# RG-LRU gates on 64 rows and two heads at a time, and weight sums of the LRU groups split during the second MLP product

## The chip, the cores and the metric

The kernel runs on one core of one Trainium2 chip. The metric is the device time of one execution in microseconds (us). The engines are TensorE (PE in the profile; PEld is its loading of weights), VectorE (DVE), ScalarE (ACT), GpSimd (POOL) and SyncE (SP, which here only issues transfers). Each engine works through its own instructions in order.

## The reference

One decoder block over 2048 tokens of width 1024, all in float32. Two mixers work side by side on one projection of the normed input, a gated short convolution (512 channels) and the Griffin block (1024 channels); after them come an output projection and an MLP of width 4096.

```python
h = rmsnorm(x, norm_mix_g)
gate_b, gate_c, v, x_r, g = split(h @ w_in)         # 512, 512, 512, 1024, 1024
y_conv = gate_b * causal_dwconv(gate_c * v, conv_w)           # 3 taps
xr = causal_dwconv(x_r, rnn_conv_w) + rnn_conv_b              # 4 taps
r = sigmoid(block_diag_linear(xr, w_a, b_a))        # 16 heads of 64 x 64
i = sigmoid(block_diag_linear(xr, w_x, b_x))
log_a = -8 * r * softplus(-lam)
a = exp(log_a)
bx = sqrt(-expm1(2 * log_a)) * (i * xr)
y_rnn = scan(h[t] = a[t] * h[t-1] + bx[t]) * gelu(g)
x = x + concat(rmsnorm(y_conv), rmsnorm(y_rnn)) @ w_out
x = x + relu(rmsnorm(x) @ w_mlp_in)^2 @ w_mlp_out
out = rmsnorm(x)
```

## The kernel before

**Products.** Each float32 operand is split into a rounded part `hi` (a cast on ACT, L166) and the remainder `lo` (a subtraction on DVE, L167), and each product is three passes over the array: hi by hi, hi by lo and lo by hi (`passes`). In the names of the profile, `w_hi` and `w_lo` are such parts of a weight, `xr_hi` and `xr_lo` those of the convolved x_r, `z_hi` those of the MLP's hidden values. One matmul multiplies 128 rows by 128 columns of weights and moves 512 tokens.

**Stages.** The tokens are worked in two halves of 1024. The first half runs `mixers_plain` (to about 420 us), the output projection, the first MLP product (`Up`), and the second one (`Down`, 822 to 1127 us, 56 steps of 24 matmuls, or 5.45 us). `Up`, `Down` and the second half's projection use a scheme of seven products in place of eight, whose order is `ORDER = (1, 2, 6, 5, 7, 3, 4)`. The second half runs `mixers_blocks` (1127 to about 1440 us), then the same stages.

**Weights of the second half.** The seven-product scheme needs four blocks of W_in in each of seven groups (groups 0 to 3 are the Griffin block's, each with x_r and g of two channel units; 4 and 5 belong to the convolution; 6 is its gate) and four sums of them. The first half leaves them in DRAM: products 1, 2 and 4 of a group as split pairs (`d_ws`), the sums of products 7, 5, 6 and 3 unsplit (`d_wk`). `mixers_blocks` fetches a split pair on POOL's queue (`wr`, three products ahead) and an unsplit sum on SP's (`wk`, four ahead), which it then splits two products ahead on ACT and DVE.

**The gates.** One unit is 128 channels, two heads. `Lru.conv` makes xr of four taps, the first on ACT (L492) and three on DVE (L500), and splits it. `Lru.gate` holds the gate matrices of the unit as 128 x 128 blocks with zeros off the diagonal: for w_a and w_x, for two blocks of 512 tokens, three passes, so 12 matmuls into two PSUM tiles `psri` (L513); then a sigmoid for each (L522, L523). `Lru.scan` follows: tanh, exp, square root on ACT, several products on DVE, one addition of 1 on ACT (L533), the scan on DVE (L537), and a copy of its state on POOL (L538). There are eight units in each half, 16 gates in all.

**Order.** PE's order is the order of the code. The other engines' orders and the transfers' are set by a scheduler at build time; tiles come from pools of fixed size, and a load or a result waits until the tile it takes over is free. In the second half the table `STEPS` puts a group's gates between the products of the next group: the first gate after product 1, its scan after 2, the second gate after 6, so two products (10.9 us) lie between them. For the first group another table applies: first gate after product 6, second after 5, one product (5.45 us) between. In the text, "group 1" means the products of group 1, with group 0's gates among them, and so on to group 4.

Of the kernel before, what the change touches and what calls it, by code (L numbers as in the profile page):

```python
# [8 lines left out]
F32 = mybir.dt.float32  # L9
F32R = mybir.dt.float32r  # L10
# [49 lines left out]
def block_kernel(  # L60
# [154 lines left out]
    def passes(s, m):  # L215
        return [(s[0], m[0]), (s[0], m[1]), (s[1], m[0])]
# [81 lines left out]
    def par(nm, i):  # L298
        return prm[:, off[nm] + i : off[nm] + i + 1]
# [182 lines left out]
    class Lru:  # L482
# [6 lines left out]
        def conv(self, xin):  # L489
            c, j = self.c, self.j  # L490
            xr = self.new("xr", (P, 2 * TB))
            nc.scalar.activation(  # L492
                xr,
                xin[:, j, 0 : 2 * TB],
                AF.Identity,
                bias=par("rnn_conv_b", c),
                scale=par("rnn_conv_w", c),
            )
            for k in range(1, 4):
                V.scalar_tensor_tensor(  # L500
                    xr, xin[:, j, k : k + 2 * TB], par("rnn_conv_w", 8 * k + c), xr, MUL, ADD
                )
            self.xr = xr
            self.split = split_new(xr, self.new, "xr")

        def gate(self, gw):
            c, j = self.c, self.j
            ps = [psum("psri") for _ in range(2)]
            for g in range(2):
                for blk in range(2):  # L510
                    pl = passes(gw, self.split)
                    for i, (ws, xs) in enumerate(pl):
                        nc.tensor.matmul(  # L513
                            ps[g][:, blk, :],
                            ws[:, j, g, :],
                            xs[:, blk * TB : blk * TB + TB],
                            start=i == 0,
                            stop=i == len(pl) - 1,
                        )
            self.r = temp("r")  # L520
            self.gi = self.new("gi")
            nc.scalar.activation(self.r, ps[0], AF.Sigmoid, bias=par("b_a", c))  # L522
            nc.scalar.activation(self.gi, ps[1], AF.Sigmoid, bias=par("b_x", c))  # L523

        def scan(self):
            c = self.c
            r, gi = (t.rearrange("p b s -> p (b s)") for t in (self.r, self.gi))
            V.tensor_mul(gi, gi, self.xr)
            v = self.xr
            nc.scalar.activation(v, r, AF.Tanh, scale=sp4[:, c : c + 1])  # L530
            nc.scalar.activation(r, r, AF.Exp, scale=sp8[:, c : c + 1])
            V.scalar_tensor_tensor(v, r, 1.0, v, ADD, MUL)
            nc.scalar.activation(r, v, AF.Identity, bias=ones[:, 0:1])  # L533
            V.scalar_tensor_tensor(v, v, 2.0, v, ADD, MUL)
            nc.scalar.activation(v, v, AF.Sqrt, scale=-1.0)
            V.tensor_mul(gi, gi, v)
            V.tensor_tensor_scan(v, r, gi, state[:, c, :], MUL, ADD)  # L537
            nc.gpsimd.tensor_copy(state[:, c, :], v[:, 2 * TB - 1 : 2 * TB])  # L538
            self.v, self.y = v, gi
# [11 lines left out]
        return acc  # L551

    def load_gate(pr):
        raw = gp.tile([P, 2, 2, P], F32, name="gate_raw")
        nc.gpsimd.dma_start(raw, gate_w[:, 2 * pr : 2 * pr + 2])
        t = temp("gate", (P, 2, 2, 2, P), F32R)
        s = (t[:, 0], t[:, 1])
        round_off(s[0], raw, s[1])
        return s
# [81 lines left out]
    def keep_sums(n):  # L641
        for i, t in weight_sums(*rawkept.pop(n)).items():
            kept[n, i] = spill("wk", t)

    def mixers_plain(h):
        acc = None
# [83 lines left out]
    class In:  # L730
# [5 lines left out]

        def fetch(self, i):
            ds = kept.pop((self.n, i))
            if i in (1, 2, 4):
                self.ready[i] = [wtile("wr", WSHAPE, F32R) for _ in range(2)]  # L740
                for t, d in zip(self.ready[i], ds):
                    nc.gpsimd.dma_start(t, d)
            else:
                self.raw[i] = refill("wk", ds, wtile)
# [113 lines left out]
    def mixers_blocks(H, more):  # L858
# [6 lines left out]
        ysB = []  # L865
        for n in range(-FETCHW, len(seq)):
            for m, sums in ((n + FETCHW, True), (n + FETCHW - 1, False)):
                if 0 <= m < len(seq) and (seq[m][1] not in (1, 2, 4)) == sums:
                    G[seq[m][0]].fetch(seq[m][1])
            m = n + LEADW  # L870
            if 0 <= m < len(seq):
                G[seq[m][0]].prepare(seq[m][1])
            if n < 0:
                continue
            s, i = seq[n]
            if s == 6 and i == 1:
                G[6].us = [G[4].u, G[5].u]
            G[s].multiply(i, H)
            G[s].drain(i)
            more(n)  # L880
            if 1 <= s <= 4:
                p = G[s - 1]
                for step in ({6: (0,), 5: (1, 2), 7: (3, 4)} if s == 1 else STEPS).get(i, ()):
                    if step == 0:
                        p.units[0].gate(p.gw)
                        p.units[1].conv(p.xin)
                    elif step == 1:
                        p.units[0].scan()
                    elif step == 2:
                        p.units[1].gate(p.gw)  # L890
                        y, acc = p.units[0].out(p.g, acc)
                        ysB.append(y)
                    elif step == 3:
                        p.units[1].scan()
                    else:
                        y, acc = p.units[1].out(p.g, acc)
                        ysB.append(y)
            if s == 6 and i == 6:
                rB = stats(acc, D, "B")
                fetched = [fetch_y(ysB, pr, 0) for pr in range(2)]  # L900
            if s == 6 and i == 7:
                early = split_y(fetched[0], "g_norm_rnn", 0)
            if s == 6 and i == 3:
                accA = conv_out(G[4].u, accA)
# [309 lines left out]
    for b in range(0, NB, 2):  # L1214
# [45 lines left out]
        with tc.manual_schedule(engines={nc.tensor.engine}):  # L1260
# [52 lines left out]
            for n in range(len(dseq) - (0 if more else 2)):  # L1313
# [14 lines left out]
                if (i, a) == (4, 0):  # L1328
                    finish(b)
                if more:  # L1330
                    if (i, a) == (5, 0):
                        load_xt(2)
                        ops2 = Operands()
# [60 lines left out]
def _lay_out(inputs):  # L1394
    import numpy as _np

    a = {n: _np.asarray(inputs[n]) for n in _INS}
    a["x_t"] = a["x"][0].T
    a["params"] = _np.concatenate([a[n].reshape(-1, P) for n, _ in ROWS]).T
    g = _np.zeros((P, NLRU, 2, P), _np.float32)  # L1400
    for n, nm in enumerate(("w_a", "w_x")):
        w = a[nm][0].reshape(NLRU, 2, 64, 64)
        for e in range(2):
            s = slice(64 * e, 64 * e + 64)
            g[s, :, n, s] = w[:, e].transpose(1, 0, 2)
    a["gate_w"] = g
    return a

# [22 lines left out]
```

## Time and profile before

| what | value |
|---|---|
| runs | 2208.73, 2209.22, 2214.24 us; median 2209.22 |
| profiled execution | 2209.43 us, of which the span of the profile is 2207.7 |
| granted clock of PE | 0.994 |
| busy: PE, weight loads, DVE, ACT, POOL | 97%, 80%, 66%, 45%, 6% of the span |
| matmuls | 9514, of them 192 at the gates |
| moved between DRAM and the core | 432 MB, 196 GB/s on average |

Busy time of PE counts a matmul from its start to its modelled end, and matmuls overlap, so the time of a row of them is read from their starts. An idle time in brackets behind a row of the timeline is that of its engine just before, with what ended it. "ACT xr_hi L166" as a releaser means that the engine waited for the cast of xr.

### The profile page before, as it was taken

The numbers are of one execution on the slowest core, as the hardware profiler recorded it, in microseconds if no ns is written. First come the engines' busy times: TensorE is split into PE (matmuls) and PEld (weight loads), VectorE is DVE, ScalarE is ACT, GpSimd is POOL, SyncE is SP. The second block draws the span as 40 slices with busy tenths as digits, with TensorE's granted clock in tenths as the row PEclk, the third lists the DMA queues.
The fourth block names the chain that finished last, engine by engine and source line by source line (L and its number), as shares of the span: only waits on it lengthen the run. The fifth ranks groups of instructions, "written<-read, shape, count | busy, mean of one in ns | idle before, by whom it ended". The sixth has DMA issues, their size and how long they took to land. (4 is left out here: it accounts for less than half of the span.)

```text
span 2207.7 us, 24962 instructions
## 1 busy us (share of the span) xinstructions
PE 2148.5 (97%) x9514; PEld 1773.1 (80%) x9514; DVE 1461.3 (66%) x1707; ACT 996.3 (45%) x1239; POOL 129.0 (6%) x224
## 2 busy tenths in 40 slices
PE   6999999999999999999999999999999999999998
PEld 5788787888887888888887778878878888888886
DVE  6577764669877785467675878456887575654446
ACT  5687813345323334343446876244543323433333
POOL 0021110000111110000010111000000000000000
PEclk9999999999999999999999999999999999999999
DMA  9654655431786788386462334655135344876431
GB/s 338 215 178 142 238 209 178 167 134 59 276 304 253 287 310 344 140 319 224 157 220 91 137 125 145 219 189 181 43 120 191 137 173 150 321 288 234 165 143 77
DMA packets 170632, 431.62 MB, mean 196 GB/s; under 512 B 14352, under 2 KB 63504, under 8 KB 170512
## 3 DMA queue, kind: packets, MB, share of 16 engines
q1 hardware_dynamic: 146416, 346.12, 43.8%
q0 software_dynamic: 21216, 74.46, 9.2%
q10 hardware_dynamic: 2880, 9.44, 1.1%
q8 instruction: 75, 1.23, 0.2%
q14 instruction: 45, 0.37, 0.0%
HBM read 292.60 MB, written 137.36 MB: 195 GB/s over the span
## 5 line engine op out<-in xcount | busy, mean ns | idle before, releaser
L770 PE MATMUL up<-H,w_hi 128*128 128x512 f32 x1792 | 554.2, 391 | 3.6 <-DVE snap L962 3.4
L167 DVE TENSOR_TENSOR w_lo<-w,w_hi 128x1024 fp32r<-128x1024 f32 x208 | 253.7, 1223 | 222.2 <-issue 120.7
L770 PEld LDWEIGHTS up<-H,w_hi 128*128 128x128 f32 x1792 | 336.8, 188 | 74.2 <-ACT H L166 4.2
L770 PE MATMUL up<-H,w_lo 128*128 128x512 f32 x896 | 350.0, 391 | 3.9 <-DVE w_lo L167 3.9
L1056 PE MATMUL dn<-w_hi,z_hi 128*128 128x512 f32 x896 | 349.7, 390 | 1.6 <-DVE x L1371 1.6
L1056 PE MATMUL dn<-w_lo,z_hi 128*128 128x512 f32 x896 | 349.3, 390 | 0.4 <-DVE w_lo L167 0.4
L1056 PE MATMUL dn<-w_hi,z_lo 128*128 128x512 f32 x896 | 349.1, 390 | 0.0
L166 ACT CAST w_hi<-w 128x1024 fp32r<-128x1024 f32 x208 | 216.5, 1050 | 195.1 <-PE dn L1056 143.3
L167 DVE TENSOR_TENSOR z_lo<-z,z_hi 128x1024 fp32r<-128x1024 f32 x112 | 136.9, 1222 | 112.1 <-issue 88.9
L770 PEld LDWEIGHTS up<-H,w_lo 128*128 128x128 f32 x896 | 168.7, 188 | 39.0 <-DVE w_lo L167 4.3
L1056 PEld LDWEIGHTS dn<-w_hi,z_hi 128*128 128x128 f32 x896 | 168.3, 188 | 37.1 <-DVE x L1371 2.4
L1056 PEld LDWEIGHTS dn<-w_lo,z_hi 128*128 128x128 f32 x896 | 168.3, 188 | 36.3 <-DVE w_lo L167 1.2
L1056 PEld LDWEIGHTS dn<-w_hi,z_lo 128*128 128x128 f32 x896 | 168.3, 188 | 35.1
L166 ACT CAST z_hi<-z 128x1024 fp32r<-128x1024 f32 x112 | 117.7, 1051 | 167.7 <-PE dn L1056 157.1
L167 DVE TENSOR_TENSOR w_lo<-raw,w_hi 128x1024 fp32r<-128x1024 f32 x76 | 92.8, 1223 | 95.3 <-ACT w_hi L166 59.5
L166 ACT CAST w_hi<-raw 128x1024 fp32r<-128x1024 f32 x76 | 79.7, 1053 | 168.7 <-PE po L241 86.7
L770 PE MATMUL in<-H,w_hi 128*128 128x512 f32 x448 | 138.7, 391 | 0.0
L949 ACT COPY snap<-up 128x1024 f32<-128x1024 f32 x48 | 48.7, 1014 | 181.1 <-PE up L770 171.1
L241 PE MATMUL po<-w_hi,y_hi 128*128 128x512 f32 x384 | 120.2, 395 | 3.5 <-ACT y_hi L621 3.5
L241 PE MATMUL po<-w_hi,y_lo 128*128 128x512 f32 x384 | 119.1, 391 | 0.2
L241 PE MATMUL po<-w_lo,y_hi 128*128 128x512 f32 x384 | 119.1, 392 | 0.0
L770 PE MATMUL in<-H,wr 128*128 128x512 f32 x504 | 116.0, 390 | 0.0
(247 smaller groups left out, 3260.0 us busy)
## 6 DMA issues: line engine op xcount, KB each, us to landing
z<-d_z SPq DMA_DIRECT2D x112, 512.0 KB, 6.7
w<-in_w_mlp_out_dram SPq DMA_DIRECT2D x80, 512.0 KB, 5.9
w<-in_w_mlp_in_dram SPq DMA_DIRECT2D x64, 512.0 KB, 4.7
d_z<-snap SPq DMA_DIRECT2D x64, 512.0 KB, 2.9
w<-d_w SPq DMA_DIRECT2D x64, 512.0 KB, 4.4
raw<-in_w_out_dram SPq DMA_DIRECT2D x48, 512.0 KB, 3.8
d_z<-z SPq DMA_DIRECT2D x48, 512.0 KB, 2.8
wr<-d_ws POOLq DMA_DIRECT2D x42, 512.0 KB, 5.3
```

What stands on the lines that cost most here:

```text
L166: nc.scalar.copy(hi, src)
L167: latest[0] = V.tensor_tensor(lo, src, hi.bitcast(F32), SUB).ins
L241: nc.tensor.matmul(ps[:, half, :], ys[:, j, t * P : (t + 1) * P], ws[j][:, 0, half * 512 : (half + 1) * 512], start=first and i == 0, stop ...
L770: nc.tensor.matmul(ps[:, j, :], ws[:, k, j * P : (j + 1) * P], hs(k), start=i in (1, 2, 5) and k == 0 and n == 0, stop=k == 3 and n == len ...
L949: nc.scalar.copy(t, ps)
L1056: nc.tensor.matmul(ps[t // 2][:, t % 2, :], zs[:, p, t * P : (t + 1) * P], ws[:, p, :], start=i in (1, 2, 5) and a == 0 and p == 0 and n == 0,
```

## The change

1. `conv`: the first tap goes from ACT to DVE, as one instruction that multiplies and adds.
2. `gate`: the matrices of one head become a 64 x 128 block, 64 columns of w_a and 64 of w_x. The two heads lie in rows 0 to 63 and 64 to 127 of the array, and each has a PSUM tile of its own. Still 12 matmuls of 512 tokens for a unit, each on 64 rows, those of the two heads next to each other.
3. Since head 0's tile has w_a's outputs in its first 64 partitions and w_x's in the others, and head 1's the other way round, there are four sigmoids on 64 partitions each, in place of two on 128. The biases of w_x are stored turned by 64.
4. The gate weights take half the memory: 128 KB a load in place of 256, and casts and remainders of 256 columns in place of 512.
5. `scan`: the addition of 1 goes from ACT to DVE.
6. `split_sums`: in the first half's second MLP product, after every third step from step 2 to step 47, one of the 16 sums of groups 0 to 3 is loaded back (SP, 512 KB), split (ACT cast, DVE subtraction) and stored as a pair (two stores of 512 KB on POOL's queue). In `mixers_blocks` these 16 then come as split pairs on POOL's queue, 32 loads in place of 16 on SP's, three products ahead, with no split there.

```diff
--- before.py
+++ after.py
@@ -489,12 +489,8 @@
         def conv(self, xin):
             c, j = self.c, self.j
             xr = self.new("xr", (P, 2 * TB))
-            nc.scalar.activation(
-                xr,
-                xin[:, j, 0 : 2 * TB],
-                AF.Identity,
-                bias=par("rnn_conv_b", c),
-                scale=par("rnn_conv_w", c),
+            V.tensor_scalar(
+                xr, xin[:, j, 0 : 2 * TB], par("rnn_conv_w", c), par("rnn_conv_b", c), MUL, ADD
             )
             for k in range(1, 4):
                 V.scalar_tensor_tensor(
@@ -506,21 +502,28 @@
         def gate(self, gw):
             c, j = self.c, self.j
             ps = [psum("psri") for _ in range(2)]
-            for g in range(2):
-                for blk in range(2):
-                    pl = passes(gw, self.split)
-                    for i, (ws, xs) in enumerate(pl):
+            head = [slice(0, 64), slice(64, P)]
+            pl = passes(gw, self.split)
+            for blk in range(2):
+                for i, (ws, xs) in enumerate(pl):
+                    for e in range(2):
                         nc.tensor.matmul(
-                            ps[g][:, blk, :],
-                            ws[:, j, g, :],
-                            xs[:, blk * TB : blk * TB + TB],
+                            ps[e][:, blk, :],
+                            ws[head[e], j, :],
+                            xs[head[e], blk * TB : blk * TB + TB],
                             start=i == 0,
                             stop=i == len(pl) - 1,
                         )
             self.r = temp("r")
             self.gi = self.new("gi")
-            nc.scalar.activation(self.r, ps[0], AF.Sigmoid, bias=par("b_a", c))
-            nc.scalar.activation(self.gi, ps[1], AF.Sigmoid, bias=par("b_x", c))
+            for e in range(2):
+                own, other = head[e], head[1 - e]
+                nc.scalar.activation(
+                    self.r[own], ps[e][own], AF.Sigmoid, bias=par("b_a", c)[own]
+                )
+                nc.scalar.activation(
+                    self.gi[own], ps[e][other], AF.Sigmoid, bias=par("b_x", c)[other]
+                )
 
         def scan(self):
             c = self.c
@@ -530,7 +533,7 @@
             nc.scalar.activation(v, r, AF.Tanh, scale=sp4[:, c : c + 1])
             nc.scalar.activation(r, r, AF.Exp, scale=sp8[:, c : c + 1])
             V.scalar_tensor_tensor(v, r, 1.0, v, ADD, MUL)
-            nc.scalar.activation(r, v, AF.Identity, bias=ones[:, 0:1])
+            V.tensor_scalar(r, v, 1.0, None, ADD)
             V.scalar_tensor_tensor(v, v, 2.0, v, ADD, MUL)
             nc.scalar.activation(v, v, AF.Sqrt, scale=-1.0)
             V.tensor_mul(gi, gi, v)
@@ -551,9 +554,9 @@
         return acc
 
     def load_gate(pr):
-        raw = gp.tile([P, 2, 2, P], F32, name="gate_raw")
+        raw = gp.tile([P, 2, P], F32, name="gate_raw")
         nc.gpsimd.dma_start(raw, gate_w[:, 2 * pr : 2 * pr + 2])
-        t = temp("gate", (P, 2, 2, 2, P), F32R)
+        t = temp("gate", (P, 2, 2, P), F32R)
         s = (t[:, 0], t[:, 1])
         round_off(s[0], raw, s[1])
         return s
@@ -641,6 +644,11 @@
     def keep_sums(n):
         for i, t in weight_sums(*rawkept.pop(n)).items():
             kept[n, i] = spill("wk", t)
+
+    def split_sums(k):
+        key = (k // 4, (7, 5, 6, 3)[k % 4])
+        t = refill("wk", kept[key])
+        kept[key] = [spill_r("ws", r, nc.gpsimd) for r in split_new(t, temp, "w")]
 
     def mixers_plain(h):
         acc = None
@@ -736,7 +744,7 @@
 
         def fetch(self, i):
             ds = kept.pop((self.n, i))
-            if i in (1, 2, 4):
+            if isinstance(ds, list):
                 self.ready[i] = [wtile("wr", WSHAPE, F32R) for _ in range(2)]
                 for t, d in zip(self.ready[i], ds):
                     nc.gpsimd.dma_start(t, d)
@@ -865,7 +873,7 @@
         ysB = []
         for n in range(-FETCHW, len(seq)):
             for m, sums in ((n + FETCHW, True), (n + FETCHW - 1, False)):
-                if 0 <= m < len(seq) and (seq[m][1] not in (1, 2, 4)) == sums:
+                if 0 <= m < len(seq) and (seq[m][0] > 3 and seq[m][1] not in (1, 2, 4)) == sums:
                     G[seq[m][0]].fetch(seq[m][1])
             m = n + LEADW
             if 0 <= m < len(seq):
@@ -1328,6 +1336,8 @@
                 if (i, a) == (4, 0):
                     finish(b)
                 if more:
+                    if n % 3 == 2 and n < 48:
+                        split_sums(n // 3)
                     if (i, a) == (5, 0):
                         load_xt(2)
                         ops2 = Operands()
@@ -1396,13 +1406,15 @@
 
     a = {n: _np.asarray(inputs[n]) for n in _INS}
     a["x_t"] = a["x"][0].T
-    a["params"] = _np.concatenate([a[n].reshape(-1, P) for n, _ in ROWS]).T
-    g = _np.zeros((P, NLRU, 2, P), _np.float32)
+    rows = {n: a[n].reshape(-1, P) for n, _ in ROWS}
+    rows["b_x"] = _np.roll(rows["b_x"], 64, axis=1)
+    a["params"] = _np.concatenate([rows[n] for n, _ in ROWS]).T
+    g = _np.zeros((P, NLRU, P), _np.float32)
     for n, nm in enumerate(("w_a", "w_x")):
         w = a[nm][0].reshape(NLRU, 2, 64, 64)
         for e in range(2):
-            s = slice(64 * e, 64 * e + 64)
-            g[s, :, n, s] = w[:, e].transpose(1, 0, 2)
+            f = e ^ n
+            g[64 * e : 64 * e + 64, :, 64 * f : 64 * f + 64] = w[:, e].transpose(1, 0, 2)
     a["gate_w"] = g
     return a
 
```

How it moves instructions, at three places. First PE at the second gate of the first half, between products of x_r (`ps_x`; `h_hi`, `h_lo` are the normed input's parts). Before:

```order
L222 MATMUL ps_x<-h_lo,w_hi 128x512
L222 MATMUL ps_x<-h_hi,w_lo 128x512
L513 MATMUL psri<-xr_hi,gate 128x512
L513 MATMUL psri<-xr_lo,gate 128x512
L513 MATMUL psri<-xr_hi,gate 128x512 x2
L513 MATMUL psri<-xr_lo,gate 128x512
L513 MATMUL psri<-xr_hi,gate 128x512 x2
L513 MATMUL psri<-xr_lo,gate 128x512
L513 MATMUL psri<-xr_hi,gate 128x512 x2
L513 MATMUL psri<-xr_lo,gate 128x512
L513 MATMUL psri<-xr_hi,gate 128x512
L222 MATMUL ps_x<-h_hi,w_hi 128x512
```

The same place in the changed kernel:

```order
L222 MATMUL ps_x<-h_lo,w_hi 128x512
L222 MATMUL ps_x<-h_hi,w_lo 128x512
L510 MATMUL psri<-xr_hi,gate 128x512 x2
L510 MATMUL psri<-xr_lo,gate 128x512 x2
L510 MATMUL psri<-xr_hi,gate 128x512 x4
L510 MATMUL psri<-xr_lo,gate 128x512 x2
L510 MATMUL psri<-xr_hi,gate 128x512 x2
L222 MATMUL ps_x<-h_hi,w_hi 128x512
```

There are twelve matmuls in both; now two neighbours are the two heads, and the third and fourth are the first to need `xr_lo`.

Next ACT in the second half, between the two gates of group 1 (`sp` holds the decay factors; L530 and L531 are tanh and exp, L533 and L534 in the changed kernel; L792, then L800, copies g from the product's PSUM). Before:

```order
L522 ACT_TABLE_LOAD
L522 ACTIVATE r<-psri,prm 128x1024
L523 ACTIVATE gi<-psri,prm 128x1024
L492 ACTIVATE xr<-xr_in,prm 128x1024
L530 ACTIVATE xr<-r,sp_335 128x1024
L531 ACT_TABLE_LOAD
L531 ACTIVATE r<-r,sp_336 128x1024
L792 COPY g<-in 128x2x512
L166 CAST xr_hi<-xr 128x1024
L533 ACTIVATE r<-xr,ones 128x1024
L563 COPY xr_in<-halo 128x2x3
L166 CAST w_hi<-wk 128x1024
```

After:

```order
L521 ACT_TABLE_LOAD
L521 ACTIVATE r<-psri,prm 64x1024
L524 ACTIVATE gi<-psri,prm 64x1024
L521 ACTIVATE r<-psri,prm 64x1024
L524 ACTIVATE gi<-psri,prm 64x1024
L800 COPY g<-in 128x2x512
L533 ACTIVATE xr<-r,sp_335 128x1024
L534 ACT_TABLE_LOAD
L534 ACTIVATE r<-r,sp_336 128x1024
L166 CAST xr_hi<-xr 128x1024
L566 COPY xr_in<-halo 128x2x3
L538 ACT_TABLE_LOAD
```

The first tap, the addition of 1 and the cast of `wk` are gone from ACT here, two sigmoids have come, and the copy of g stands ahead of tanh and exp instead of behind them.

Last DVE in the second half, ahead of the second gate of group 2 (L787, then L795, adds the second product to x_r; L528, then L531, multiplies the gate by xr; L532, then L535, follows exp). Before:

```order
L528 TENSOR_TENSOR gi<-gi,xr 128x1024
L500 SCALAR_TENSOR_TENSOR xr<-xr_in,prm,xr 128x1024
L787 TENSOR_TENSOR xr_in<-in,xr_in 128x2x512
L500 SCALAR_TENSOR_TENSOR xr<-xr_in,prm,xr 128x1024 x2
L532 SCALAR_TENSOR_TENSOR xr<-r,xr 128x1024
L167 TENSOR_TENSOR xr_lo<-xr,xr_hi 128x1024
L167 TENSOR_TENSOR w_lo<-wk,w_hi 128x1024
L534 SCALAR_TENSOR_TENSOR xr<-xr 128x1024
L167 TENSOR_TENSOR w_lo<-wk,w_hi 128x1024
```

After:

```order
L492 TENSOR_SCALAR xr<-xr_in,prm 128x1024
L795 TENSOR_TENSOR xr_in<-in,xr_in 128x2x512
L496 SCALAR_TENSOR_TENSOR xr<-xr_in,prm,xr 128x1024
L531 TENSOR_TENSOR gi<-gi,xr 128x1024
L496 SCALAR_TENSOR_TENSOR xr<-xr_in,prm,xr 128x1024 x2
L535 SCALAR_TENSOR_TENSOR xr<-r,xr 128x1024
L167 TENSOR_TENSOR xr_lo<-xr,xr_hi 128x1024
L536 TENSOR_SCALAR r<-xr 128x1024
L537 SCALAR_TENSOR_TENSOR xr<-xr 128x1024
```

The addition of the second product and the product by the gate, which needs all four sigmoids, now stand ahead of two of the taps, and so of xr.

## The prediction

> **What bounds the kernel now.** I read the head of the page first, then the chain, then the table of waits of the matmul engine, then the groups of the lines that the diff touches, and last the timeline at single gates.
>
> ```profile
> span 2207.7 us, 24962 instructions
> PE 2148.5 (97%) x9514; PEld 1773.1 (80%) x9514; DVE 1461.3 (66%) x1707; ACT 996.3 (45%) x1239; POOL 129.0 (6%) x224
> ```
>
> PE is busy for 97% of the span, and 59 us are not PE's. So two things can move the time: fewer or shorter matmuls, and those 59 us. The table of waits (engine, line, waited for: us in total, times, longest) says who owns the gates' part of them:
>
> ```profile
> PE bc L368 <- DVE diag L361: 10.0, 2, 9.3
> PE psri L513 <- ACT xr_hi L166: 8.3, 3, 3.1
> PE psri L513 <- DVE xr_lo L167: 7.7, 7, 2.4
> ```
>
> The gate matmuls (psri) wait 16 us, for the cast of xr and for its remainder. Nothing in the change touches the first line.
>
> **The gate's matmuls.** One gate without a wait, on PE's timeline (start, duration):
>
> ```profile
> 126.54 0.39 PE L513 MATMUL psri<-xr_hi,gate 128*128 128x512 f32 x1
> 126.76 0.39 PE L513 MATMUL psri<-xr_lo,gate 128*128 128x512 f32 x1
> 126.99 0.62 PE L513 MATMUL psri<-xr_hi,gate 128*128 128x512 f32 x2
> ...
> 129.26 0.39 PE L222 MATMUL ps_x<-h_hi,w_hi 128*128 128x512 f32 x1
> ```
>
> Twelve matmuls from 126.54 to 129.26 are 2.72 us, 0.227 each; the 0.39 is latency that overlaps. The changed gate still issues twelve, each 512 columns long, but on 64 rows, in pairs of two heads on the two halves of the array, in two PSUM tiles. A gate gets shorter only if the two of a pair run at the same time. No row of before shows that. If they do, the floor is the issue of two weight loads and two matmuls, whose price the sums of squares show, since their matmuls have one column:
>
> ```profile
> 321.90 1.98 PEld L606 LDWEIGHTS sps<-ones,xr 128*128 128x128 f32 x16
> 322.13 1.84 PE L606 MATMUL sps<-ones,xr 128*128 128x1 f32 x16
> ```
>
> Sixteen in 1.84 to 1.98 us: 0.12 us for one, 0.24 for a pair, hardly over the 0.227 of one long matmul. Six pairs of 0.24 are 1.44 instead of 2.72: 1.28 us less per gate, **-20.5 us** over 16 gates. The other end is 0: pairs one after the other, 2.72 as now.
>
> Going from 128-row to 64-row matmuls and back may empty the array. By the rows above that costs between nothing and, twice, the 0.16 by which the latency outlasts the pitch plus a weight load that no matmul covers (0.12): 0 to 0.56 per gate. I take 0.35, nearer the upper end because both switches happen in every gate: 16 x 0.35 = **+5.6** (0 to +9). The bare matmul part is -15, between -20.5 and, without overlap, +9.
>
> The Trainium skill ("TensorE: Matmul & The Clock Gate", Part 3 on packing small matmuls) says that tiles in different row groups run concurrently, with 3.07 times measured for four tiles of 32 rows; for two tiles that points to the overlap I take. The same skill ("TensorEngine Tiling (Array Packing)", tiling modes) says that a change of mode drains TensorE and gives no figure; it speaks for the +5.6. By the first alone the sum below would be -22, with the second it stays near -16. No row of before shows either.
>
> **What ACT and DVE gain and lose.** Groups (busy, mean ns) and, for the sigmoids, two rows of the timeline:
>
> ```profile
> L492 ACT ACTIVATE xr<-xr_in,prm 128x1024 f32<-128x1024 f32 x16 | 19.8, 1239 | 6.6 <-DVE xr_in L796 6.2 <-DMA d_y<-gi 0.4
> L533 ACT ACTIVATE r<-xr,ones 128x1024 f32<-128x1024 f32 x16 | 18.3, 1145 | 1.8 <-DVE xr L532 1.6
> L583 DVE TENSOR_SCALAR u<-cv,prm 128x1024 f32<-128x1024 f32 x8 | 5.7, 750 | 0.4 <-POOL haloc L579 0.4
> L166 ACT CAST w_hi<-wk 128x1024 fp32r<-128x1024 f32 x28 | 29.1, 1047 | 27.1 <-PE in L770 14.7 <-DVE w_lo L167 6.0 <-issue 4.3
> L167 DVE TENSOR_TENSOR w_lo<-wk,w_hi 128x1024 fp32r<-128x1024 f32 x28 | 34.0, 1223 | 14.8 <-ACT w_hi L166 7.2 <-PE in L770 5.8 <-issue 1.9
> ...
> 1186.36 1.12 ACT L522 ACTIVATE r<-psri,prm 128x1024 f32<-128x1024 f32 x1
> 1187.37 1.11 ACT L523 ACTIVATE gi<-psri,prm 128x1024 f32<-128x1024 f32 x1
> ```
>
> Per gate unit, ACT loses the first tap (1.24) and the +1 (1.15), which DVE takes at 0.71 each (5.7 over 8; the nearest row). ACT gains two sigmoids: four on 64 partitions instead of two on 128, each still 1024 long. I take the pitch of 1.01 for each, since the length is unchanged; if half the partitions halved it, the gain would be 0. So ACT stays about level (-2.4 + 2.0), DVE pays +1.4, that is +11.6 in each half. In the second half the 16 splits of raw sums leave as well: ACT -16.8 (16 x 1.047), DVE -19.6 (16 x 1.223). The gate weights are half as big; their eight loads and casts are off PE's path and I cost them at nothing.
>
> Is there cover? Windows (length, PE, PEld, DVE, ACT, POOL, clock, DMA share, GB/s) of the first mixers, of the second product of the first half, and of the second mixers:
>
> ```profile
> 77.00:280.00 203.00, 198.56 (x871) 163.25 (x872) 144.78 (x130) 160.15 (x174) 28.12 (x37) 1.00 0.54 188
> 840.00:870.00 30.00, 30.00 (x134) 24.83 (x134) 16.36 (x15) 11.36 (x12) 0.00 (x0) 1.00 0.97 381
> 880.00:1120.00 240.00, 240.00 (x1057) 198.17 (x1056) 150.10 (x168) 99.44 (x117) 6.07 (x12) 1.00 0.57 204
> 1180.00:1380.00 200.00, 185.97 (x789) 150.51 (x788) 155.85 (x126) 155.07 (x147) 25.11 (x39) 0.97 0.40 135
> ```
>
> In the first mixers DVE goes from 145 to some 155 of 203 us, in the second it falls, ACT falls there from 155 to about 137. No engine becomes a bound by its sum; order decides, gate by gate.
>
> **First mixers, waits at gates.** PE, with the idle time and its releaser in brackets:
>
> ```profile
> 77.41 0.73 PE L513 MATMUL psri<-xr_hi,gate 128*128 128x512 f32 x2 [2.05 <-ACT xr_hi L166]
> 177.10 0.50 PE L513 MATMUL psri<-xr_lo,gate 128*128 128x512 f32 x1 [0.95 <-DVE xr_lo L167]
> 241.34 0.50 PE L513 MATMUL psri<-xr_lo,gate 128*128 128x512 f32 x1 [1.40 <-DVE xr_lo L167]
> ```
>
> The four taps now run on one engine, the first 0.5 us shorter and without a turn in ACT's queue, so xr is ready 0.5 to 2 us earlier; I take 2.5 of these 4.4 us back: **-2.5** (0 to -4.4).
>
> **Second mixers, waits at gates.** Here the second gate of a group follows one product (5.45 us, 24 x 0.227) or two (10.9) after the first, and the cast for it stands in ACT's queue behind the first gate's work. Two places in the old order, PE first, then ACT between them:
>
> ```profile
> 1195.28 0.50 PE L513 MATMUL psri<-xr_hi,gate 128*128 128x512 f32 x1 [3.13 <-ACT xr_hi L166]
> 1196.54 0.79 PE L513 MATMUL psri<-xr_lo,gate 128*128 128x512 f32 x1 [0.76 <-DVE xr_lo L167]
> 1200.67 0.62 PE L770 MATMUL in<-H,w_hi 128*128 128x512 f32 x2
> ...
> 1287.94 0.51 PE L513 MATMUL psri<-xr_hi,gate 128*128 128x512 f32 x1 [3.08 <-ACT xr_hi L166]
> 1294.26 1.06 PE L770 MATMUL in<-H,w_hi 128*128 128x512 f32 x2
> ...
> 1189.77 1.15 ACT L530 ACTIVATE xr<-r,sp 128x1024 f32<-128x1024 f32 x1 [0.16 <-DVE gi L528]
> 1190.94 1.28 ACT L531 ACT_TABLE_LOAD   x1
> 1192.24 1.15 ACT L531 ACTIVATE r<-r,sp 128x1024 f32<-128x1024 f32 x1
> 1193.29 0.99 ACT L792 COPY g<-in 128x1024 f32<-128x1024 f32 x1
> 1194.18 1.04 ACT L166 CAST xr_hi<-xr 128x1024 fp32r<-128x1024 f32 x1
> ```
>
> At group 1 PE was free at 1192.15, and left the gate at 1200.67: 8.52 for 2.72 of work, so 5.8 lost (its matmuls came 0.43 apart for 3 us after that wait). At group 3 likewise: 1284.86 to 1294.26, 6.7 lost. By the new order of group 1: PE free 1.28 earlier, 1190.87; four sigmoids from 1186.36 to 1190.4, the copy of g (0.9, waits for the product's end) to 1191.8, tanh 1.17, table 1.30, exp 1.05, cast 1.04: xr_hi at 1196.4, xr_lo 1.2 later, and then five pairs, slow again: out at 1199.5 and 1.2 us of slow matmuls behind them. That is 8.4 lost: +2.6. At groups 2 and 4 the cast now stands behind four sigmoids, tanh, table and exp as well, and xr_lo behind a product's drain on DVE: 8.6 us of ACT from the first sigmoid, which starts 1.3 us after the gate, plus 1.2 for the remainder and two to four for what DVE has ahead: 13 to 15 after the gate against 10.9 of products. I take 4.1 for each (0 to 6) where 0.8 and 0 stand now: +7.4. At group 3 the cast now comes ahead of tanh: -6.7. The first gate of group 2 waits for xr_lo (row below), and DVE has less ahead of it without the splits: -2.2; two others -0.7.
>
> ```profile
> 1225.23 0.51 PE L513 MATMUL psri<-xr_lo,gate 128*128 128x512 f32 x1 [2.38 <-DVE xr_lo L167]
> ```
>
> Together +2.6 + 7.4 - 6.7 - 2.2 - 0.7 = **+0.4** (-9 to +8).
>
> **The splits moved into the second MLP product.** Sixteen times, every third step (5.45 us each), SP loads 512 KB, ACT casts, DVE subtracts, POOL's queue stores 2 x 512 KB: 24 MB over 261 us is 94 GB/s on top of 204, below the 381 that the window at 840 carries. DVE gets 19.6 us on 150 of 240, ACT 16.8 on 99. PE never waits in that window, 240.00 of 240. I cost it at **+0.5** (0 to +4): the cover is the z and weight tiles fetched four steps ahead; with it gone, the next thing late would be a z load. Back in the second mixers, 32 loads of split sums go to POOL's queue in place of 16 raw ones on SP's:
>
> ```profile
> wr<-d_ws POOLq DMA_DIRECT2D x42, 512.0 KB, 5.3
> wk<-d_wk SPq DMA_DIRECT2D x28, 512.0 KB, 4.3
> ```
>
> They land in 5.3 us and are issued two to three products (over 10 us) ahead, so nothing is added. POOL runs in order: a load that waits for its tile holds up the copies of the scan's state and halo behind it; 28 us of POOL in 203 leaves room, and I cost that at 0, with +3 as its other end.
>
> **Sum.** -20.5 + 5.6 - 2.5 + 0.4 + 0.5 = -16.5. The profiled execution took 2209.43 us (span 2207.7), the median of the runs is 2209.22, so they agree: 2209.2 - 16.5 = 2192.7, say 2193.
>
> **Rivals.** *The pairs don't overlap.* For it: all matmuls of before follow each other at 0.227, and none is shown side by side. Then the -20.5 is 0 and the switches still cost: 5.6 - 2.5 + 0.4 + 0.5 = +4, 2213 (2208 to 2217). Chance 0.16. *The cast on ACT gives it back*, the one that ends slower: xr_hi stands behind four sigmoids, tanh, table and exp at the second gates of groups 1 to 4. If each loses 9 us, group 1's 8.4 everywhere, there are 36 where 13.3 stand now, +23 in place of +2.6 + 7.4 - 6.7: the sum is +3, 2212, and with group 1's waits lengthened by the slow clock to 11 each it is 2220. It decides from about 8.3 us lost per second gate. Against it: three of the four have two products to hide in, or the cast ahead of tanh. Chance 0.12. *Everything works*: no cost at the switch and no waits at groups 2 and 4: -16.5 - 5.6 - 7.4 = -29.5, 2180 (to 2185). For it: the 0.24 of a pair is above 0.227 already, so issue may hide the switch. Chance 0.12. My forecast, 2185 to 2203, has 0.60.
>
> **How the numbers follow.** A measurement of this kernel tells about 0.3%, 6.6 us, from no change. Faster than 2202.6: forecast and the third rival, 0.72, less 0.02 at the forecast's edge: 0.70. The first rival lies mostly within the bound (0.11 of 0.16), the second half (0.06): with the edge 0.19 the same; 0.11 slower. The range 2183 to 2213 leaves out some 0.08 below and 0.09 above.
>
> **What would show it.** Pairs: gate matmuls of two heads starting 0.01 to 0.12 apart, a gate without waits in 1.4 to 2.0 us, and PE's busy time less by about 15. If instead a gate is still 2.7 long, the first rival. Splits: 240 of 240 PE in the second product. Casts: idle time before the second gates of groups 1, 2 and 4 of 4 to 6 us, at group 3 none. Sigmoids near 1.1 us on 64 partitions. I would be wrong most cheaply by the switch, which no row prices.

## The result, and the profile after

The changed kernel takes 2199.93 us (median of 4, 2198.12 to 2201.91) against 2210.61 (2208.73 to 2214.24) on the same chip: ratio 0.995, 95% interval 0.9933 to 0.9967, 10.7 us less. The profiled execution took 2200.14, of which the span is 2198.3. The head of the page:

```profile
span 2198.3 us, 25153 instructions
PE 2138.3 (97%) x9514; PEld 1755.2 (80%) x9514; DVE 1481.1 (67%) x1739; ACT 994.7 (45%) x1238; POOL 165.9 (8%) x288
```

PE's busy time fell by 10.2 us; the time outside it is 60.0 where it was 59.2. One gate without a wait, on PE's timeline:

```profile
123.44 0.39 PE L222 MATMUL ps_g<-h_hi,w_lo 128*128 128x512 f32 x1
123.76 0.50 PE L510 MATMUL psri<-xr_hi,gate 64*128 64x512 f32 x2
124.10 0.40 PE L510 MATMUL psri<-xr_lo,gate 64*128 64x512 f32 x2
124.33 0.63 PE L510 MATMUL psri<-xr_hi,gate 64*128 64x512 f32 x4
124.80 0.39 PE L510 MATMUL psri<-xr_lo,gate 64*128 64x512 f32 x2
125.03 0.40 PE L510 MATMUL psri<-xr_hi,gate 64*128 64x512 f32 x2
125.35 0.50 PE L222 MATMUL ps_x<-h_hi,w_hi 128*128 128x512 f32 x1
```

Two matmuls of two heads are one row (x2), and the next row starts 0.23 us later; at both switches, and behind the first pair, 0.1 us is added. From the start of the last matmul ahead of the gate to the start of the first behind it are 1.91 us. Before, it was 2.95, from this row to the 129.26 shown above:

```profile
126.31 0.39 PE L222 MATMUL ps_g<-h_hi,w_lo 128*128 128x512 f32 x1
```

That is 1.04 less, 16.6 over 16 gates without a wait. The table of waits of PE shows what came against it (the waits of PE that the change can touch):

```profile
PE psri L510 <- ACT xr_hi L166: 11.1, 3, 5.5
...
PE psri L510 <- DVE xr_lo L167: 2.4, 5, 0.7
...
PE psri L510 <- ACT gi L524: 2.1, 2, 1.6
PE ps_x L222 <- ACT gi L524: 1.8, 3, 0.6
...
PE in L778 <- ACT g L800: 1.4, 1, 1.4
...
PE ps_c L222 <- ACT gi L524: 0.6, 1, 0.6
```

The waits for the cast grew from 8.3 to 11.1, those for the remainder fell from 7.7 to 2.4, and the rows with gi as releaser are new: PE waits for a PSUM tile (PSUM holds the sums of the matmuls until another engine has read them) that the last sigmoid has not read yet. The groups of the moved work, by line:

```profile
L521 ACT ACTIVATE r<-psri,prm 64x1024 f32<-64x1024 f32 x32 | 35.6, 1113 | 0.5
L524 ACT ACTIVATE gi<-psri,prm 64x1024 f32<-64x1024 f32 x32 | 35.6, 1112 | 0.5
L492 DVE TENSOR_SCALAR xr<-xr_in,prm 128x1024 f32<-128x1024 f32 x16 | 12.9, 809 | 5.8 <-ACT xr_in L671 5.8
L536 DVE TENSOR_SCALAR r<-xr 128x1024 f32<-128x1024 f32 x16 | 11.0, 688 | 0.1
```

A sigmoid on 64 partitions takes 1.11 us, as one on 128 did. For the stages I take the first and last starts of a product's matmuls (`po`, `up`, `dn`, `in`), from rows of the timeline by tile such as these two of the changed kernel:

```profile
L241 PE MATMUL po<-w_hi,y_hi x384: 389/389/499, 361.8 to 1571.4; 128*128 128x512 f32 x192
L778 PE MATMUL in<-H,wr x888: 387/389/793, 1124.9 to 1433.0; 128*128 128x512 f32 x178
```

The first mixers end where `po` begins, the second mixers last from the first to the last `in`. The whole table, with the experiments' kernels by their labels (profiled executions in columns 3 to 6, us):

| kernel | median | first mixers | first MLP product | second MLP product | second mixers |
|---|---|---|---|---|---|
| before | 2209.9 to 2210.7 | 367.5 | 314.7 | 307.1 | 311.4 |
| changed | 2199.9 | 361.8 | 316.3 | 306.7 | 308.1 |
| gates_only | 2217.1 | 371.2 | 313.4 | 307.4 | 314.6 |
| moves_only | 2203.8 | 360.0 | 315.9 | 306.6 | 311.5 |
| splits_only | 2204.6 | 367.9 | 316.3 | 306.6 | 303.6 |
| no_gates | 2189.8 | 359.6 | 315.8 | 306.9 | 300.5 |
| same_rows | 2214.4 | 364.8 | 314.6 | 306.7 | 320.9 |
| head_by_head | 2200.2 | 363.6 | 314.5 | 306.6 | 308.3 |
| two_sigmoids | 2197.0 | 365.5 | 313.9 | 306.6 | 302.3 |
| conv_first | 2203.0 | 362.3 | 317.3 | 306.7 | 309.5 |
| four_sigmoids | 2213.4 | 363.2 | 314.3 | 306.7 | 321.6 |
| edges | 2192.3 | 357.9 | 316.2 | 306.6 | 303.0 |
| ng_edges | 2194.1 | 361.2 | 314.5 | 306.6 | 304.7 |
| edges_w2 | 2188.5 | 356.9 | 314.4 | 306.6 | 300.7 |

The first MLP product differs by up to 4 us between kernels that do the same in it, so that column says nothing of the change. The medians of the experiments are from sessions of their own, each beside the kernel before, which is why ratios are given below.

### The profile page after: what moved, and what is told of

The parts are those of the page before. It is cut to its first block, busy times and chain, and to the rows that moved or that the text cites. A ratio compares the mean times of both kernels' runs of the same rounds, so it can differ in the third digit from the quotient of the medians.

```text
span 2198.3 us, 25153 instructions
## 1 busy us (share of the span) xinstructions
PE 2138.3 (97%) x9514; PEld 1755.2 (80%) x9514; DVE 1481.1 (67%) x1739; ACT 994.7 (45%) x1238; POOL 165.9 (8%) x288
## 4 chain that ended last, share of the span: by engine, by line
PE 78%; DVE 12%; ACT 4%; DMA 3%; issue 3%; SPq 0%; POOL 0%; DVEq 0%; ACTq 0%; POOLq 0%
PE dn L1064 28%; PE up L778 21%; PE po L241 11%; PE in L778 10%; PE ps_b L222 2%; PE ps_v L222 2%; PE ps_c L222 2%; DMA w<-in_w_mlp_out_dram 1%; DVE w_lo L167 1%; DVE xr L496 1%; DVE xr L540 1%; DMA xq<-in_x_dram 1%; PE psri L510 1%; PE ps_x L222 1%; DVE H L167 1%
## 5 line engine op out<-in xcount | busy, mean ns | idle before, releaser
L778 PE MATMUL in<-H,wr 128*128 128x512 f32 x888 | 206.1, 393 | 1.4 <-ACT g L800 1.4
L778 PEld LDWEIGHTS in<-H,wr 128*128 128x128 f32 x888 | 167.4, 189 | 39.6 <-ACT g L800 1.8
```

The source lines that it names most:

```text
L778: nc.tensor.matmul(ps[:, j, :], ws[:, k, j * P : (j + 1) * P], hs(k), start=i in (1, 2, 5) and k == 0 and n == 0, stop=k == 3 and n == len ...
```

## The experiments

**The parts one by one.** *gates_only* has parts 2 to 4 of the change, *moves_only* parts 1 and 5, *splits_only* part 6, and *no_gates* parts 1, 5 and 6; the code of each is that of the diff above.

> The kernel before with the 64-row gates, their four sigmoids and halved weights alone (parts 2 to 4); first tap, addition of 1 and the splits stay where they were. Theory (pairs of heads run side by side, 1.04 us less per clean gate, and the four sigmoids give part of it back): 16.6 us of matmul time goes, but ACT gets 17.6 us more in each half with nothing taken off, so the waits at the gates grow by some 10 to 14: 2204 to 2210, -1 to -7 against before. Rival (the gain comes from the work taken off ACT and DVE, not from the pairs): 2212 to 2220, slower than before.

> The kernel before with the first tap and the addition of 1 on DVE alone (parts 1 and 5). Theory: the 4.4 us of waits for xr in the first mixers go, in the second mixers 1 to 4 us: 2203 to 2207, -4 to -8. Rival (the gain comes from the work taken off ACT): -8 to -11, as much as the whole change.

> The kernel before with the 16 splits moved into the second MLP product alone (part 6). Theory: the second product stays without a wait of PE; in the second mixers the 2.4 us of waits for w_lo and a part of the 11.6 at the gates go: -2 to -6, 2205 to 2209. Rival (24 MB more in the second product cost PE waits there): +2 to +6.

> The changed kernel with the old gates of 128 rows and two sigmoids (parts 1, 5 and 6 alone). Theory: the changed kernel has 16.6 us less of gate matmuls than this, and about 10 us more of waits that the four sigmoids make, so this one stands some 3 to 8 us above the changed kernel: 2203 to 2208. Rival (all of the gain is the moves and the splits): 2200, as the changed kernel.

Measured, as ratios to before: gates_only 1.003 (1.0019 to 1.0041), moves_only 0.9975 (0.9963 to 0.9986), splits_only 0.9976 (0.9965 to 0.9987), no_gates 0.9912 (0.9898 to 0.9925). So the packed gates, with the sigmoids that they need, make the kernel slower, alone by 7 us and on top of the other parts by 10 (2189.8 to 2199.9). My theory had them as the gain; for gates_only and no_gates it missed, and the rival, that the gain is the work taken off ACT and DVE, stands, though no_gates gained twice what its rival said (2200). In gates_only the wait for the cast is the largest of PE, 23.3 us where it was 8.3:

```profile
PE psri L514 <- ACT xr_hi L166: 23.3, 6, 6.3
```

moves_only fell into the range of its theory (2203 to 2207), splits_only 0.4 us below its own (2205 to 2209). The moves work in the first mixers (-7.5 us in the table), the splits in the second (-7.8), and together they are worth 20 us, where the two alone give 6.2 and 5.4. Of these 8.6 us more, 3.2 lie in the second mixers (-10.9, against +0.1 and -7.8); where the rest comes from was not found. no_gates has 6.8 us of waits for xr at its gates, where before had 16.0:

```profile
PE psri L509 <- ACT xr_hi L166: 4.5, 1, 4.5
...
PE psri L509 <- DVE xr_lo L167: 2.3, 4, 0.7
```

**What the pairs are worth.** same_rows puts both heads on the same rows (it leaves out the second head's own matrix and channels), head_by_head takes the loop over the heads outside:

```diff
-    ws[head[e], j, :], xs[head[e], blk * TB : blk * TB + TB]
+    ws[head[0], j, :], xs[head[0], blk * TB : blk * TB + TB]      # same_rows

-    for blk in range(2):
-        for i, (ws, xs) in enumerate(pl):
-            for e in range(2):
+    for e in range(2):                                            # head_by_head
+        for blk in range(2):
+            for i, (ws, xs) in enumerate(pl):
```

> The changed kernel, but both heads' matmuls use rows 0 to 63 of the array (the second head's output is then that of the first head's block, which is not what the reference computes); number, size and order of matmuls, loads and sigmoids stay. Theory (two neighbours overlap because they lie in different rows): a pair takes 2 x 0.227, a clean gate 2.72 + 0.3, 1.3 us more: 16 gates, of which three wait anyway, +17 to +21, so 2217 to 2221. Rival (the 64-row matmul is short by itself, in whatever rows): 2200.

> The changed kernel with the loop over the heads outside: six matmuls of the first head, then six of the second. Theory (only neighbours in PE's queue overlap): one pair of twelve overlaps, a clean gate takes 2.5 + 0.3; its first PSUM tile is done 1.3 us before the second, so its sigmoids start earlier, which gives 2 to 5 us of waits back: +12 to +18, 2212 to 2218. Rival (the two halves run their own queues and catch up whatever the order): 2200.

same_rows took 2214.4 us, 14.5 more than the changed kernel. Its gate without a wait, on PE's timeline:

```profile
126.01 0.39 PE L222 MATMUL ps_g<-h_hi,w_lo 128*128 128x512 f32 x1
126.33 0.73 PE L510 MATMUL psri<-xr_hi,gate 64*128 64x512 f32 x2
126.90 0.63 PE L510 MATMUL psri<-xr_lo,gate 64*128 64x512 f32 x2
127.37 1.08 PE L510 MATMUL psri<-xr_hi,gate 64*128 64x512 f32 x4
...
129.29 0.50 PE L222 MATMUL ps_x<-h_hi,w_hi 128*128 128x512 f32 x1
```

3.28 us from 126.01 to 129.29 against 1.91: the overlap needs different rows, and is worth 1.37 us a gate, 22 over 16, of which 14.5 reach the time. Longer gates leave ACT more time: the changed kernel's waits for gi (4.5 us) and for the copy of g (1.4) are not in its table of waits. The theory holds; the expected 2217 to 2221 was too high by that.

head_by_head took 2200.2, like the changed kernel, where I expected 2212 to 2218. Its gate:

```profile
1277.84 0.39 PE L778 MATMUL in<-H,wr 128*128 128x512 f32 x1
1278.15 0.49 PE L510 MATMUL psri<-xr_hi,gate 64*128 64x512 f32 x1
1278.49 0.39 PE L510 MATMUL psri<-xr_lo,gate 64*128 64x512 f32 x1
1278.72 0.63 PE L510 MATMUL psri<-xr_hi,gate 64*128 64x512 f32 x3
1279.07 0.51 PE L510 MATMUL psri<-xr_lo,gate 64*128 64x512 f32 x2
1279.30 0.62 PE L510 MATMUL psri<-xr_hi,gate 64*128 64x512 f32 x3
1279.76 0.39 PE L510 MATMUL psri<-xr_lo,gate 64*128 64x512 f32 x1
1279.99 0.39 PE L510 MATMUL psri<-xr_hi,gate 64*128 64x512 f32 x1
1280.31 0.50 PE L778 MATMUL in<-H,wr 128*128 128x512 f32 x1
```

2.47 us, between 1.91 and 2.95. In the code the first head has hi, lo, hi, hi, lo, hi and only then the second. The row of three hi at 1278.72 lasts 0.63 us, of which 0.39 is the last one's latency, so the three start within 0.24 us, and one head has only two there: the second head's matmuls run before the first head's are through. So pairs need not be neighbours in the code: the theory missed in mechanism and time, and the rival (2200) has the time, though the heads catch up only in part. The trace has the starts and not the place of a matmul in the program, so it does not tell whether the engine or the build mixes the heads. The half microsecond a gate that it loses is 9 us over 16 gates. About half of it came back in waits: those for the cast are 6.3 us in it (11.1) and those for gi 0.6 (4.5), but those for xr_lo 4.5 (2.4) and for the copy of g 2.7 (1.4). The rest is not accounted for.

**The sigmoids.** two_sigmoids takes two sigmoids on 128 partitions in the changed kernel (it leaves out that the two heads' outputs lie the other way round), four_sigmoids cuts those of no_gates into four:

```diff
-    for e in range(2): ...                                        # two_sigmoids
+    nc.scalar.activation(self.r, ps[0], AF.Sigmoid, bias=par("b_a", c))
+    nc.scalar.activation(self.gi, ps[1], AF.Sigmoid, bias=par("b_x", c))

+    for g, (t, b) in enumerate(((self.r, par("b_a", c)), (self.gi, par("b_x", c)))):
+        for s in (slice(0, 64), slice(64, P)):                    # four_sigmoids
+            nc.scalar.activation(t[s], ps[g][s], AF.Sigmoid, bias=b[s])
```

> The changed kernel with two sigmoids on 128 partitions in place of four on 64 (the second heads' halves of r and i then sit in the wrong place, which is not what the reference computes). Theory (a sigmoid costs by its length, not by its partitions, so four hold the PSUM tiles 2 us longer and put the cast 2 us later): the 4.5 us of waits for PSUM in the first mixers go and the three second gates wait 2 us less each: -8 to -12, 2188 to 2192. Rival (ACT has room, the sigmoids cost nothing): 2200.

> The kernel without the 64-row gates (gates of 128 rows, with the moves and the splits; 2189.8), but each of its two sigmoids cut into two of 64 partitions. Matmuls and PSUM tiles stay. Theory A (a sigmoid costs by its length, 1.1 us on 64 partitions as on 128, so the cut alone puts 2.1 to 2.5 us more on ACT between the gate and the cast for the next one, and holds PSUM longer): +6 to +14, 2196 to 2204, of it 5 to 9 in the second mixers. Theory B (the sigmoids are covered; what costs is the 64-row matmul and its PSUM tiles by heads): 2188 to 2192.

four_sigmoids took 2213.4 us, 23.6 more than no_gates, with the same matmuls and PSUM tiles. 21 of them lie in the second mixers, where its waits of PE are now

```profile
PE psri L509 <- ACT xr_hi L166: 12.5, 4, 5.6
...
PE psri L509 <- DVE xr_lo L167: 6.1, 9, 0.9
```

So theory A has the right sign and place, and its 6 to 14 was too small: each of the second gates waits (5.6, 2.1, 2.1 and 2.8 us), and behind such a wait the gate's matmuls come 0.43 us apart (at group 1):

```profile
1194.20 0.80 PE L509 MATMUL psri<-xr_hi,gate 128*128 128x512 f32 x1 [5.61 <-ACT xr_hi L166]
...
1199.67 0.62 PE L509 MATMUL psri<-xr_lo,gate 128*128 128x512 f32 x1
1200.10 0.42 PE L509 MATMUL psri<-xr_hi,gate 128*128 128x512 f32 x1
```

From the last matmul ahead of a gate to the first behind it, the eight gates of the second mixers take 52.5 us, where those of no_gates take 33.6.

two_sigmoids, though, came to 2197.0, 3 below the changed kernel and not 8 to 12: second mixers -5.8, but first mixers +3.7, with one wait of 3.1 us for xr_lo that the changed kernel does not have, under another order of the scheduler's. With it, the four kernels that share the moves and the splits form a square (medians, us):

| | two sigmoids | four sigmoids |
|---|---|---|
| gates of 128 rows | 2189.8 (no_gates) | 2213.4 (four_sigmoids) |
| packed gates | 2197.0 (two_sigmoids) | 2199.9 (changed) |

The prices do not add. Four sigmoids cost 23.6 us with the old gates and 3.0 with the packed ones; the packed matmuls give 13.5 us with four sigmoids and lose 7.1 with two. Only the two together have one price, +10.1. Why packed matmuls lose with two sigmoids was not settled; the waits for xr at the gates are 16.1 us there and 6.8 in no_gates. Each of these kernels also got another order on ACT and DVE from the scheduler, so a step in this square is the price of an edit together with the order that it brought.

**The order on ACT and DVE.** In the changed kernel at group 1 (ACT, DVE, then PE):

```profile
1181.81 1.11 ACT L521 ACTIVATE r<-psri,prm 64x1024 f32<-64x1024 f32 x1
1185.18 1.11 ACT L524 ACTIVATE gi<-psri,prm 64x1024 f32<-64x1024 f32 x1
1191.17 1.03 ACT L166 CAST xr_hi<-xr 128x1024 fp32r<-128x1024 f32 x1
...
1186.33 1.23 DVE L531 TENSOR_TENSOR gi<-gi,xr 128x1024 f32<-128x1024 f32 x1 [5.69 <-ACT gi L524]
1187.47 1.28 DVE L496 SCALAR_TENSOR_TENSOR xr<-xr_in,prm,xr 128x1024 f32<-128x1024 f32 x1
...
1192.26 0.79 PE L510 MATMUL psri<-xr_hi,gate 64*128 64x512 f32 x2 [5.54 <-ACT xr_hi L166]
```

DVE stands idle for 5.69 us in front of the product that needs the fourth sigmoid, and the last tap of the second unit's xr, which needs no gate, waits behind it; then the cast waits behind tanh and exp. In the first mixers, at the sixth gate:

```profile
181.69 1.06 ACT L550 ACTIVATE xr<-gi 128x1024 f32<-128x1024 f32 x1 [5.08 <-POOL state L541]
182.83 1.05 ACT L166 CAST xr_hi<-xr 128x1024 fp32r<-128x1024 f32 x1
185.19 1.11 ACT L521 ACTIVATE r<-psri,prm 64x1024 f32<-64x1024 f32 x1
...
187.48 0.49 PE L510 MATMUL psri<-xr_hi,gate 64*128 64x512 f32 x1 [1.60 <-ACT gi L524]
```

ACT is idle for 5.08 us in front of a square of y that waits for POOL's copy of the state, while the sigmoids of a gate that ended at 174.3 stand behind it; the next gate finds no PSUM tile. conv_first swaps two calls; edges sets the order itself, given here in short form (units 0 and 1 are the two of a group; in the first mixers it also calls the convolution of unit 1 after the gate of unit 0); ng_edges does a part of it in the second mixers of no_gates; edges_w2 adds one edge to edges:

```diff
-    p.units[0].gate(p.gw)
-    p.units[1].conv(p.xin)
+    p.units[1].conv(p.xin)                                        # conv_first
+    p.units[0].gate(p.gw)

     # edges: behind(late, early) orders two instructions of one engine
+    behind(tanh of unit 0, cast of unit 1); behind(gi * xr of unit 0, xr_lo of unit 1)
+    behind(sigmoids of unit 1, square root of unit 0)
+    group 1: behind(third sigmoid of unit 0, cast of unit 1); behind(copy of g, cast of unit 1)
+    first mixers: behind(cast of unit 1, sigmoids of unit 0); behind(square of y, sigmoids of unit 0)
     # edges_w2
+    group 4, product 3: behind(third sigmoid of the last unit, cast of the weights)
```

> The changed kernel with the second unit's convolution and cast called ahead of the first unit's gate in the second mixers, two lines swapped. Theory (the cast of xr behind four sigmoids, tanh, table and exp on ACT makes the second gates of groups 1, 2 and 4 wait 5.5, 2.8 and 2.8 us, with the remainder and the slow clock after it 18 us): those waits go, -10 to -16, 2184 to 2190. Rival (another thing is late behind the cast, such as the PSUM tiles that the sigmoids hold): 2197 to 2203.

> The changed kernel, same instructions, with order alone set on ACT and DVE around the gates: in the second mixers the second unit's cast stands ahead of the first unit's tanh (for the first group also ahead of two sigmoids and of the copy of g), its remainder ahead of the first unit's product by the gate, its sigmoids behind the first unit's square root; in the first mixers the first unit's sigmoids stand ahead of the second unit's cast and of the square of y. Theory A (the packed gates lose their gain to the order on ACT and DVE, not to the amount of work): the waits of 5.5, 2.8 and 2.8 us with remainder and slow clock (18 us) go for the most part, and the 4.5 us for PSUM: second mixers from 308 to 293 to 298 us, first from 362 to 354 to 358, in all 2180 to 2190. Theory B (the amount of ACT's work, 1.1 us for each of 64 sigmoids, is the cause): other waits take their place, 2196 to 2204.

> The kernel without the 64-row gates (128 rows, two sigmoids, moves and splits; 2189.8) with the same order in the second mixers alone. Theory A (order): its one long wait at a second gate, 4.5 us with 0.7 for the remainder and the slow clock behind it, goes: -4 to -8, 2182 to 2186. Theory B (that wait is ACT's work, not its order): 2188 to 2192.

> The kernel with the changed instructions and the order set (2192.3), and one edge more: the cast of the weights for the third sum of group 4 ahead of the last two sigmoids of the last unit, where PE waited 6.0 us for that cast. Theory A (order): 3 to 5 of the 6.0 us go, and with them the slow clock behind them: second mixers from 303.0 to 297 to 300 us, in all 2186 to 2190, beside the 2189.8 of the kernel without the packed gates. Theory B (the tile that the cast writes is free only then, or the work only moves): 2191 to 2195.

conv_first took 2203.0, at the upper end of its rival: the waits for the cast fell to 1.3 us, but others came (6.2 us for a copy of cv, 5.7 for gi, 4.9 for g). edges took 2192.3, 7.6 below the changed kernel with the same instructions. That lies between its two theories (2180 to 2190, 2196 to 2204): order matters, as A says, but less than A said, and one wait of 6.0 us took the place of some of those removed:

```profile
1331.31 1.03 ACT L166 CAST w_hi<-wk 128x1024 fp32r<-128x1024 f32 x1
1332.39 1.22 PE L804 MATMUL in<-H,w_hi 128*128 128x512 f32 x2 [6.02 <-ACT w_hi L166]
```

edges_w2 puts that cast ahead of two sigmoids, as its theory A said; the wait fell to 2.7 us and the time to 2188.5 (ratio 0.9905, 0.9889 to 0.9922), 11.4 below the changed kernel:

```profile
PE in L804 <- ACT w_hi L166: 2.7, 1, 2.7
```

That is the lowest of all, though not told apart from no_gates (0.9912, 0.9898 to 0.9925): with the order set, the packed gates no longer lose, and no gain of theirs is shown. ng_edges took 2194.1, 4 above no_gates and above both its theories. It does not settle what order is worth with two sigmoids, since it has only three of the edges (tanh behind the cast, the product by the gate behind the remainder, and at group 1 the copy of g behind the cast): the second unit's sigmoids are not set behind the first unit's square root in it, nor a sigmoid of the first unit behind the cast at group 1.

## Why the prediction was right, and where it was not

2193 was forecast, inside 2183 to 2213, and faster; 2199.9 was measured. That the total came near is in part luck. The forecast has about -5 us for the gates (-20.5 + 5.6 + 2.6 + 7.4) and about -12 for the moves and the splits (-2.5 - 6.7 - 2.2 - 0.7 + 0.5). By no_gates the gates are +10 and the rest -20: two misses against each other, and the sign of the gates was wrong. By its steps:

- *Pairs, -20.5, and switches, +5.6.* Right for the matmuls: -15 was the sum, -16.6 by gates without a wait. In time it is -13.5 with four sigmoids on both sides and +7.1 with two, so the forecast was wrong to pass it on whole; PE's busy time fell by 10.2 where about 15 was named as the sign. The switch cost 0.3 us a gate where I took 0.35. The Trainium skill's rule that tiles in different row groups run concurrently ("TensorE: Matmul & The Clock Gate", Part 3) agrees with the trace, 1.91 us a gate against 3.28 on the same rows.
- *ACT "stays about level".* This is the step that failed. The sum is right over the whole span (busy 996 to 995 us; from 1180 to 1380 us ACT is busy 144.5, where I had about 137), but it was summed over the stage and should have been placed in the queue: four sigmoids come 1.12 us apart, 4.5 us where two took 2.1, between a gate and everything that the next gate needs. Cut so with the old gates they cost 23.6 us, in the changed kernel 3.0 against two_sigmoids, and setting the order takes 11.4 back with all four kept; so the amount and the order cost together, and their shares stay open. I had it only inside the +2.6 and +7.4 of the second mixers.
- *Second gates of groups 1, 2 and 4, lost 8.4, 4.1, 4.1; group 3, none.* Right in place and near in size: waits of 5.5 and 0.7, 2.8 and 0.7, 2.8 and 0.7 with slow matmuls behind them, and none at group 3. Two of the three waits for the cast are shorter than the 4 to 6 us named as the sign.
- *First mixers, -2.5 beside the matmuls.* Two errors against each other. The moves alone give 7.5 there, not 2.5; and the waits for PSUM behind the sigmoids (2.1, 1.8 and 0.6 us in the table of waits) were not foreseen: I asked what the casts wait for, not how long a gate holds its tiles.
- *The splits, +0.5 in the second product and their relief inside the +0.4.* No wait of PE in the second product, as said:

```profile
876.00:1116.00 240.00, 240.00 (x1057) 198.13 (x1056) 165.01 (x181) 110.73 (x129) 20.13 (x38) 1.00 0.79 294
```

  294 GB/s stand where 204 were: 90 more, by the estimate 94. But the relief in the second mixers is 7.8 us by itself and 10.9 with the moves.
- *The rivals.* That the pairs don't overlap is refuted. That the cast on ACT gives it back, given 0.12, is near to what happened to the packed gates taken alone: gates_only is slower, with waits of 6.3, 3.9, 4.2 and 4.2 us for the cast at all four second gates. The total came out faster because the other parts carry it.

## What to carry to other kernels

When PE work is packed, price what the packing does to the engine that drains it: here 16.6 us of matmuls came with 32 activations more, of full length, in the one queue that feeds the next gate, and in the order that the scheduler gave them the two together lost 10 us. Busy sums by stage do not show this; write the in-order queue between one consumer and the next and count what stands ahead. Before a step is dropped, set that order by hand: here it took 11.4 us off with the same instructions. Price a part with its partner present and absent; where the two prices differ, as 23.6 and 3.0 do, neither is the part's own. And run each part alone and left out: the whole change looked like a gain of its headline, and its headline, as scheduled, was the loss.

## What the runs showed of the hardware

Pairs of 64-row matmuls on different rows pass at 0.23 us a pair, and on the same rows nearly one after the other (1.91 and 3.28 us a gate). They overlap in part even when the code has all six of one head ahead of the other's (2.47 us a gate); over how many instructions that reaches was not tried. An activation on 64 partitions takes 1.11 us as on 128, and four in a row start 1.12 us apart (1181.81 to 1185.18), while two on 128 partitions started 1.01 apart; why, stays open.
